# Scores with transposes or outputs behind them in one block of weights, and products' matmuls in written order

## The chip, the cores and the metric

The kernel runs on one core of a Trainium2 chip. The metric is the device time of one execution in microseconds, as the median of several runs. The engines that matter here are TensorE (PE in the profile, with its weight loads as PEld), VectorE (DVE), ScalarE (ACT), and SP, whose queue starts the transfers of the weights.

## The reference

A hybrid encoder of two layers on 256 tokens, width 2048, in float32. Cut to what matters:

```python
for i in range(DEPTH):                       # 2 layers
    h = rmsnorm(x, g_mix[i])
    z = h @ w_in[i]                          # dq, dk, dv, cq, ckv, kr, gate a, gate b
    # differential attention: 8 heads, two softmax maps of 64 columns each
    weights = softmax(q0 @ k0.T / 8) - lam * softmax(q1 @ k1.T / 8)
    od = rmsnorm(weights @ v, g_subln[i]) * (1 - lam_init)
    # latent attention: 8 heads, 128 + 64 (rotary) columns
    qf = rmsnorm(cq) @ w_q_up[i];  kvf = rmsnorm(ckv) @ w_kv_up[i]
    om = softmax((q_nope @ k_nope.T + q_rope @ k_rope.T) * scale) @ v_mla
    m = sigmoid(ga) * (od @ w_branch_diff[i]) + sigmoid(gb) * (om @ w_branch_mla[i])
    x = x + m @ w_out[i]
    x = x + (silu(g) * u) @ w_down[i]        # g, u = rmsnorm(x) @ w_gate_up[i], width 5632
    x = x + sigmoid(rmsnorm(x) @ w_ple_gate[i]) * (p[i] @ w_ple_in[i])
return rmsnorm(x, g_final)
```

## The kernel before, in words

Features lie on the 128 partitions and the 256 tokens along the free axis. A weight matrix is read from memory once per layer in pieces of 128 x 1024 floats (`piece`, at most eight blocks each), each of which ACT rounds to `whi` (L204) and DVE turns into the remainder `wlo` (L81, by the helper `tt`). Three buffers hold `whi` pieces and three `wlo` pieces. The activations are held the same way, as a hi and a lo half side by side in one tile of 512 columns: `ua` and `ub` are sixteen such tiles each.

A product of one output tile (`product`, or `pair` for two short ones) is a series of *blocks*, made in `emit`: for each input tile j a *lead*, hi weights times both halves of the tile (L229, 512 columns), and a *rest*, lo weights times the hi half (L233, 256 columns). Both add into one PSUM bank `mm`. Most products have 16 blocks. `blocks` lists the (lead, rest) pairs of a layer from the first queries on; it is emptied at that place in each layer.

The stages of a layer are: the values of the differential attention (`values`), the latents, queries and keys of eight heads with the attention of the heads before them (`pipelined`, with `beside` giving it products to fill in), latent attention with the gates as filling, the two branch products with `w_bd` and `w_bm`, `w_out`, the gated feed-forward in three parts of 14, 14 and 16 tiles (`FF_PARTS`), each followed by its share of `w_down`, and the last gate `w_pg`. `w_out` reads the merged tiles from `ua`, and `w_down` reads the feed-forward's tiles from `ua`. Every one of these tiles comes out of a short chain: ACT copies half of a bank (`joined`, L260), DVE adds the other half (L81), one or two DVE operations follow, and `split` writes the hi half by ACT (L268) and the lo half by DVE (L81).

Smaller matmuls stand among the blocks. Each head has scores S (L436, 12 matmuls of 64 rows for the differential heads, 10 of 128 rows for the latent ones), transposes of its weights T (L455, four), and outputs O (L729, four in the differential heads). N are the two matmuls that spread a norm over the partitions (L345). `settle` transposes the normalised outputs of a differential head, two transposes each (L745), and splits them. T, O, N and the transposes of `settle` write PSUM banks of the tag `at`, of which there are two; S writes banks of the tag `S`, also two.

The order of the instructions of each engine comes from a planner that simulates a timeline (`schedule_with_timeline_sim=True`) and takes what is ready first; dependencies without semaphores (`NO_SYNC`) can be added by hand to force an order on one engine. `PLACES` does so: an entry ("S", 6, 265) puts the scores of head 6 into block 265, that is behind its lead, ahead of its rest and ahead of the next block's lead. Between the entries of one block no order is given, and nothing else orders a block against the block before it.

`queries_keys(h, *inside)` can run a function inside step 8 of a product: the norms of the latents and, in `latent_norm`, the matmuls N.

Of the kernel before, what the change touches and what calls it, by code (L numbers as in the profile page):

```python
# [19 lines left out]
P = 128  # L20
T = 256
# [6 lines left out]
KVR = 256  # L28
# [14 lines left out]
GAPS = {("fa", 0): (8, 0), ("fc", 0): (48, 0), ("fa", 7): (0, 16)}  # L43
KR_GAP = 56
FIRST = 7
PLACES = (("N", 0, 24), ("N", 1, 56), ("S", 0, 65), ("S", 1, 112), ("T", 0, 112), ("S", 2, 148), ("T", 1, 148), ("S", 3, 176), ("T", 2, 176), ("S", 4, 210), ("T", 3, 210),
          ("S", 5, 234), ("T", 4, 234), ("O", 4, 240), ("S", 6, 265), ("O", 5, 272), ("T", 6, 296), ("S", 7, 297), ("T", 7, 337), ("O", 7, 361),
          ("S", 8, 416), ("S", 9, 432), ("T", 8, 438))
NO_SYNC = mybir.DependencyInfo(mybir.DependencyClass.NoSync, mybir.DependencyReason.DATA)

TWO_PI = 2.0 * math.pi
# [8 lines left out]
def encoder(ctx, tc, x, p, positions, cols, lams, wq, wk, wv, wcq, wckv, wkr, wga, wgb,  # L60
            w_q_up, w_kn, w_v, w_bd, w_bm, w_out, w_gate, w_up, w_down, w_pin, w_pg, rope_c, out):
    nc = tc.nc
    V, A, PE = nc.vector, nc.scalar, nc.tensor
# [10 lines left out]
    def scratch(tag, bufs, n=T):  # L74
        return tmp.tile([P, n], F32, tag=tag, name=tag, bufs=bufs)

    def bank(ps=ps_at, tag="at", name="at", shape=(P, 2 * T)):
        return ps.tile(list(shape), F32, tag=tag, name=name)

    def tt(o, a, b, op):  # L80
        return V.tensor_tensor(out=o, in0=a, in1=b, op=op)  # L81
# [8 lines left out]
    ua = [const.tile([P, 2 * T], F32R, name=f"ua{j}") for j in range(NC)]  # L90
# [27 lines left out]
    def g(name, i=0):  # L118
        return gcol[:, off[name] + i : off[name] + i + 1]


    ident = const.tile([P, P], F32, name="ident")
# [63 lines left out]
    def piece(src, n, high=0, low=0):  # L186


        w = wts.tile([P, PT * P], F32, tag="w32", name="w32", bufs=W_BUFS)
        lo = wts.tile([P, PT * P + 64], F32R, tag="wlo", name="wlo", bufs=3)[:, low : low + PT * P]  # L190
        if not step:
            step.append(wts.tile([P, STEP], F32, tag="step", name="step", bufs=1))
            nc.gpsimd.memset(step[0], 0.0)
        hi = wts.tile([P, PT * P + 64], F32R, tag="whi", name="whi", bufs=3)[:, high : high + PT * P]
        srcs = src if isinstance(src, list) else [src]
        m = n * P // len(srcs)
        for k, src in enumerate(srcs):
            dst = w[:, k * m : (k + 1) * m]
            if len(src.shape) == 3:
                dst = dst.rearrange("p (a b) -> p a b", a=src.shape[1])  # L200
            nc.sync.dma_start(dst, src)
        for k in range(len(srcs)):
            s = slice(k * m, (k + 1) * m)
            last_split[:] = A.activation(hi[:, s], w[:, s], AF.Copy), tt(lo[:, s], w[:, s], hi[:, s].bitcast(F32), ALU.subtract)  # L204
        if chores:
            with after_splits():
                chores.pop(0)()
        return hi, lo
# [8 lines left out]
    last_split, last_mm, chores, sq0, step, blocks = [], [], [], [], [], []  # L217
# [8 lines left out]
    def emit(acc, hi, lo, at, us, first, last, inside=None):  # L226
        for j, u in enumerate(us):
            s, start, stop = slice((at + j) * P, (at + j + 1) * P), first and j == 0, last and j == len(us) - 1
            lead = PE.matmul(acc, hi[:, s], u, start=start, stop=False)  # L229
            if inside and inside[0] == j:  # L230
                with tc.issue_after(lead.ins):
                    inside[1]()
            rest = PE.matmul(acc[:, T:], lo[:, s], u[:, :T], start=False, stop=stop)  # L233
            blocks.append((lead.ins, rest.ins))
            if inside and inside[0] == j:
                tc.keep_in_program_order(rest)

    def product(src, us, inside=None):


        acc = bank(ps_mm, "mm", "mm")
        n = len(us)
        for a in range(0, n, PT):
            m = min(PT, n - a)
            hi, lo = piece(src[:, a * P : (a + m) * P], m)
            emit(acc, hi, lo, 0, us[a : a + m], a == 0, a + m == n, inside and (inside[0] - a, inside[1]))
        return acc
# [10 lines left out]
    def joined(acc, o=None):  # L258
        t = scratch("join", 3)
        A.activation(t, acc[:, T:], AF.Copy)  # L260
        o = scratch("a", 4) if o is None else o
        tt(o, acc[:, :T], t, ALU.add)
        return o

    def split(u, src, gain=None):
        hi, lo = u[:, :T], u[:, T:]
        if gain is None:
            return A.activation(hi, src, AF.Copy), tt(lo, src, hi.bitcast(F32), ALU.subtract)  # L268
        return A.activation(hi, src, AF.Copy, scale=gain), stt(lo, src, gain, hi.bitcast(F32), ALU.mult, ALU.subtract)

    def rsqrt(src, n, eps, width):

        v, y, a = (stat.tile([P, 2 * DH], F32, tag="r" + s, name="r" + s, bufs=2)[:, :width] for s in "vya")
        ts(v, src, 1.0 / n, eps, ALU.mult, ALU.add)
        ts(y.bitcast(I32), v.bitcast(I32), -0.5, 1597463007.0, ALU.mult, ALU.add)
        for _ in range(3):
            stt(a, y, -0.5, y, ALU.mult, ALU.mult)
            tt(a, a, v, ALU.mult)
            stt(y, a, 1.5, y, ALU.add, ALU.mult)
        return y  # L280
# [52 lines left out]
    def norm(sums, n):  # L333

        s = bank()
        for j, a in enumerate(sums):
            for b in range(2):
                PE.matmul(s[:, b : b + 1], a[:, b * P : (b + 1) * P], ones[:, 0:1], start=j + b == 0, stop=j + b == len(sums))
        return rsqrt(s[:, 0:2], n, EPS, 2)
# [130 lines left out]
    def weights(tag="E", dt=F32):  # L470
        return tmp.tile([P, 2, T], dt, tag=tag, name=tag, bufs=2)

    groups = {"N": [], "S": [], "T": [], "O": []}

    def place(kind, n, block):


        lead, rest = blocks[block]
        for i in groups[kind][n]:
            for late, early in ((i, lead), (rest, i), (blocks[block + 1][0], i)):  # L480
                tc.add_manual_dep(late, early.name, NO_SYNC, reason="inside a block")

    last_exp = [None]
    SWAP16 = [(j + 16) % 32 for j in range(32)]
# [62 lines left out]
    for L in range(DEPTH):  # L547
# [44 lines left out]

        def queries_keys(h, *inside):
            for which, w in enumerate((wq, wk)):
                a = joined(product(w[L, h], ua, inside=(8, inside[which]) if inside and inside[which] else None))
                sh = scratch("sh", 2)
                V.stream_shuffle(sh, a, ROPE16)
                tt(sh, sh, sr, ALU.mult)
                tt(a, a, cr, ALU.mult)
                tt(a, a, sh, ALU.add)  # L600
                split(qk[h][which], a)


        cq, ckv = ub[8:12], ub[12:14]
# [9 lines left out]
        def latent_norm(us, gain, raws, col, behind=False):  # L614
            rl = spread(col, behind)
            for c in range(len(us)):
                stt(raws[c], raws[c], g(f"{gain}{L}", c), rl, ALU.mult, ALU.mult)
                split(us[c], raws[c])
# [20 lines left out]
        rq, rkv = raws[:4], raws[4:]  # L639
        skv = latent(ckv, wckv, rkv)  # L640
        sq = latent(cq, wcq, rq)
        lcols = []

        def norm_and_latent(sq):
            lcols.append(norm([sq], QR))
            latent_norm(ckv, "g_kv_latent", rkv, lcols[0], True)

        blocks.clear()
        for group in groups.values():
            group.clear()  # L650
        queries_keys(0, lambda: lcols.append(norm([skv], KVR)), lambda: norm_and_latent(sq))
        queries_keys(1, None, lambda: latent_norm(cq, "g_q_latent", rq, lcols[1]))

        def beside():

# [40 lines left out]
        gas, gbs, early = [], [], []  # L696
# [40 lines left out]
        def settle(h0):  # L737

            rd = rsqrt(ssd[:, 2 * h0 : 2 * h0 + 8], P, SUB_EPS, 8)
            for h in range(h0, h0 + 4):  # L740
                t = bank()
                for b in range(2):
                    o, j = od[h][:, b * P : (b + 1) * P], 2 * (h - h0) + b
                    ts(o, o, rd[:, j : j + 1], None, ALU.mult)
                    PE.transpose(t[:, b * P : (b + 1) * P], o, ident)  # L745
                split(ods[h], t[:, :T], gsub[:, L : L + 1])

        def pipelined(weigh, put, heads, step):
# [38 lines left out]
            split(oms[h], o[:, :T])  # L787

        pipelined(mla_weights, mla_out, MH, fill_gate)
        for kind, n, block in PLACES:  # L790
            place(kind, n, block)

        for n in todo:
            gate(wgb, gate_b, n - NC)
# [28 lines left out]
        for part, (f0, f1) in enumerate(FF_PARTS):  # L823
            for f in range(f0, f1):
                a = pre.pop(0) if pre else joined(product(w_gate[L, f], ub))
# [5 lines left out]
                b = pre.pop(0) if pre else joined(product(w_up[L, f], ub))  # L831
# [26 lines left out]
        for n in range(NC - 2 * final):  # L858
            a = pre.pop(0) if pre else joined(product(w_pg[L, n], ub))
# [15 lines left out]
    parts, banks, tiles_ = {}, {}, {}  # L875
# [14 lines left out]
    for n in ends:  # L890
        m = banks[n, 1] = bank(ps_mm, "mm", "mm")
        for j in range(whole[n], NC):
            w = slice(j % PT * P, (j % PT + 1) * P)
# [185 lines left out]
```

## Time and profile before

| | |
|---|---|
| median of 3 runs | 2825.02 us (2824.64 to 2825.53) |
| profiled execution, its own time | 2824.55 us |
| its span in the profile | 2822.7 us, 43984 instructions |
| mean granted clock of TensorE | 1.00 |
| DVE busy | 2079.6 us, 74% |
| ACT busy | 1533.2 us, 54% |
| matmuls of L229, on ub and on ua | 3936 and 3712 |
| HBM read | 526.39 MB, 187 GB/s over the span |

A row of the timeline has the start and the duration in us from the span's start, the engine, the line, the operation, what it writes and reads by the program's names without numbers, its shape and how many are merged into the row. In brackets stands the idle time ahead of it and what ended it, where there was any. Starts of PE rows are recorded; their ends are modelled and overlap the next start. A row of the wait list has the waiter, what it waited for, us in total, times, and the longest.

### The profile page before, as it was taken

The numbers are of one execution on the slowest core, as the hardware profiler recorded it, in microseconds if no ns is written. First come the engines' busy times: TensorE is split into PE (matmuls) and PEld (weight loads), VectorE is DVE, ScalarE is ACT, GpSimd is POOL, SyncE is SP. The second block draws the span as 40 slices with busy tenths as digits, with TensorE's granted clock in tenths as the row PEclk, the third lists the DMA queues.
The fourth block names the chain that finished last, engine by engine and source line by source line (L and its number), as shares of the span: only waits on it lengthen the run. The fifth ranks groups of instructions, "written<-read, shape, count | busy, mean of one in ns | idle before, by whom it ended". The sixth has DMA issues, their size and how long they took to land.

```text
span 2822.7 us, 43984 instructions
## 1 busy us (share of the span) xinstructions
PE 2815.3 (100%) x16691; PEld 2490.4 (88%) x16691; DVE 2079.6 (74%) x3566; ACT 1533.2 (54%) x2554; POOL 3.1 (0%) x17
## 2 busy tenths in 40 slices
PE   9999999999999999999999999999999999999999
PEld 8888988888888888888888889888888888888888
DVE  8898668776666666677869976687766666666777
ACT  7676546554444444455646765465544444444555
POOL 0000000000000000000000000000000000000000
PEclk9999999999999999999999999999999999999999
DMA  7545455555665565565564454555556655655664
GB/s 247 175 162 172 158 186 198 193 194 194 187 200 193 188 194 198 193 194 193 195 192 167 157 172 158 193 198 193 194 194 189 199 193 184 202 194 193 193 193 157
DMA packets 158180, 531.36 MB, mean 188 GB/s; under 512 B 17168, under 2 KB 25360, under 8 KB 157968
## 3 DMA queue, kind: packets, MB, share of 16 engines
q1 hardware_dynamic: 157536, 527.96, 56.8%
q8 instruction: 131, 2.15, 0.3%
q10 hardware_dynamic: 432, 0.59, 0.1%
q14 instruction: 81, 0.66, 0.1%
HBM read 526.39 MB, written 2.10 MB: 187 GB/s over the span
## 4 chain that ended last, share of the span: by engine, by line
PE 100%; DVE 0%; DVEq 0%; issue 0%
PE mm L229 61%; PE mm L233 31%; PE S L436 1%; PE mmv L522 1%; PE mmv L523 1%; PE mmv L521 1%; PE at L455 1%; PE at L729 1%; PE mm L878 0%; PE at L786 0%; PE mm L422 0%; PE at L537 0%; PE at L745 0%; PE mmv L492 0%; PE at L345 0%; PE at L311 0%
## 5 line engine op out<-in xcount | busy, mean ns | idle before, releaser
L204 ACT ACTIVATE whi<-w 128x1024 fp32r<-128x1024 f32 (+2 forms) x1038 | 1064.1, 1026 | 1209.5 <-issue 576.6
L81 DVE TENSOR_TENSOR wlo<-w,whi 128x1024 fp32r<-128x1024 f32 (+2 forms) x1038 | 1225.2, 1181 | 638.1 <-ACT whi L204 627.8
L229 PE MATMUL mm<-ub,whi 128*128 128x512 f32 x3936 | 1339.6, 389 | 0.0
L229 PE MATMUL mm<-ua,whi 128*128 128x512 f32 x3712 | 1273.6, 390 | 0.0
L233 PE MATMUL mm<-ub,wlo 128*128 128x256 f32 x3936 | 1086.5, 276 | 0.0
L233 PE MATMUL mm<-ua,wlo 128*128 128x256 f32 x3712 | 1028.5, 278 | 0.0
L229 PEld LDWEIGHTS mm<-ub,whi 128*128 128x128 f32 x3936 | 737.9, 188 | 152.0
L229 PEld LDWEIGHTS mm<-ua,whi 128*128 128x128 f32 x3712 | 696.2, 188 | 140.6
L233 PEld LDWEIGHTS mm<-ub,wlo 128*128 128x128 f32 x3936 | 738.7, 188 | 1.0
L233 PEld LDWEIGHTS mm<-ua,wlo 128*128 128x128 f32 x3712 | 696.9, 188 | 2.1
L81 DVE TENSOR_TENSOR a<-mm,join 128x256 f32<-128x256 f32 (+1 forms) x423 | 174.0, 416 | 1.7 <-ACT join L907 1.4
L260 ACT ACTIVATE join<-mm 128x256 f32<-128x256 f32 x452 | 165.6, 369 | 4.0 <-PE mm L233 3.4
L81 DVE TENSOR_TENSOR xT<-xT,mm 128x256 f32<-128x256 f32 x256 | 106.8, 420 | 41.5 <-PE mm L233 37.6
L81 DVE TENSOR_TENSOR a<-a,row 128x256 f32<-128x256 f32 (+1 forms) x209 | 87.8, 421 | 6.0
L81 DVE TENSOR_TENSOR a<-a 128x256 f32<-128x256 f32 x120 | 51.0, 425 | 4.0
L81 DVE TENSOR_TENSOR ua<-a,ua 128x256 fp32r<-128x256 f32 x120 | 50.1, 417 | 1.0 <-ACT ua L268 1.0
L446 ACT ACTIVATE E<-S,nm 128x256 f32<-128x256 f32 x96 | 44.2, 473 | 11.9 <-DVE nm L87 11.6
L268 ACT ACTIVATE ua<-a 128x256 fp32r<-128x256 f32 x120 | 48.4, 404 | 2.6 <-DVE a L81 2.6
L521 PE MATMUL mmv<-whi,ua 128*128 128x512 f32 x124 | 47.0, 391 | 0.0
L522 PE MATMUL mmv<-whi,ua 128*128 128x512 f32 x124 | 47.0, 392 | 0.0
L523 PE MATMUL mmv<-wlo,ua 128*128 128x512 f32 x124 | 41.2, 391 | 0.0
L81 DVE TENSOR_TENSOR ssq<-ssq,sq 128x256 f32<-128x256 f32 x96 | 40.0, 417 | 0.3 <-ACT sq L298 0.3
(214 smaller groups left out, 1209.6 us busy)
## 6 DMA issues: line engine op xcount, KB each, us to landing
w<-in_w_gate SPq DMA_DIRECT2D x176, 512.0 KB, 4.6
w<-in_w_up SPq DMA_DIRECT2D x176, 512.0 KB, 4.6
w<-in_w_down SPq DMA_DIRECT2D x128, 512.0 KB, 4.2
w<-in_wga SPq DMA_DIRECT2D x64, 512.0 KB, 3.8
w<-in_wgb SPq DMA_DIRECT2D x64, 512.0 KB, 3.7
w<-in_w_out SPq DMA_DIRECT2D x64, 512.0 KB, 4.5
w<-in_w_pg SPq DMA_DIRECT2D x64, 512.0 KB, 4.6
w<-in_w_down SPq DMA_DIRECT2D x64, 384.0 KB, 3.6
```

The lines of the kernel that those rows point to most:

```text
L81: return V.tensor_tensor(out=o, in0=a, in1=b, op=op)
L204: last_split[:] = A.activation(hi[:, s], w[:, s], AF.Copy), tt(lo[:, s], w[:, s], hi[:, s].bitcast(F32), ALU.subtract)
L229: lead = PE.matmul(acc, hi[:, s], u, start=start, stop=False)
L233: rest = PE.matmul(acc[:, T:], lo[:, s], u[:, :T], start=False, stop=stop)
L260: A.activation(t, acc[:, T:], AF.Copy)
L268: return A.activation(hi, src, AF.Copy), tt(lo, src, hi.bitcast(F32), ALU.subtract)
L436: group.append(PE.matmul(S[:, b, :], q[:, b * P : (b + 1) * P], k, start=j == 0, stop=j == len(pairs) - 1).ins)
L446: last_exp[0] = A.activation(E[:, b, :], S[:, b, :], AF.Exp, bias=nm[:, b : b + 1], scale=scale, accum_out=sm[:, b : b + 1])
L455: group.append(PE.transpose(tp[:, kb, b * P : (b + 1) * P], W[:, b, kb * P : (kb + 1) * P], ident).ins)
L521: PE.matmul(banks[k][b], xh, hi[:, s], start=c == 0, stop=False)
L522: PE.matmul(banks[k][b], xl, hi[:, s], start=False, stop=False)
L523: last_mm[:] = [PE.matmul(banks[k][b], xh, lo[:, s], start=False, stop=c == n - 1)]
```

## The change

It has three parts. `emit` adds two dependencies without semaphores per block, so that each lead stands behind the rest of the block written before it, and each rest behind its own lead, through the whole program; `blocks` is no longer emptied, and each layer counts from `base`. `PLACES` becomes a table from block to names, and `place` strings the names of a block in the order given: lead, first name, second name, ..., rest. And the entries differ: S0 goes from block 65 to 59 and N1 from 56 to 59 behind it; S6 from 265 and O5 from 272 to 268 together; T6 from 296 to 297 behind S7 and ahead of F0; F4 to F7 (the transposes of `settle`, which had no place) to 424, 425, 432 and 435; S10 and T9, which had none, to 480. The function inside the second head's keys runs at step 11 instead of 8.

```diff
-PLACES = (("N", 0, 24), ("N", 1, 56), ("S", 0, 65), ("S", 1, 112), ("T", 0, 112), ("S", 2, 148), ("T", 1, 148), ("S", 3, 176), ("T", 2, 176), ("S", 4, 210), ("T", 3, 210),
-          ("S", 5, 234), ("T", 4, 234), ("O", 4, 240), ("S", 6, 265), ("O", 5, 272), ("T", 6, 296), ("S", 7, 297), ("T", 7, 337), ("O", 7, 361),
-          ("S", 8, 416), ("S", 9, 432), ("T", 8, 438))
+PLACES = {24: ["N0"], 59: ["S0", "N1"], 112: ["S1", "T0"], 148: ["S2", "T1"], 176: ["S3", "T2"], 210: ["S4", "T3"], 234: ["S5", "T4"],
+          240: ["O4"], 268: ["S6", "O5"], 297: ["S7", "T6", "F0"], 337: ["T7"], 361: ["O7"], 416: ["S8"], 424: ["F4"], 425: ["F5"],
+          432: ["F6", "S9"], 435: ["F7"], 438: ["T8"], 480: ["S10", "T9"]}
...
             rest = PE.matmul(acc[:, T:], lo[:, s], u[:, :T], start=False, stop=stop)
+            if blocks:
+                behind(lead.ins, blocks[-1][1])
+            behind(rest.ins, lead.ins)
             blocks.append((lead.ins, rest.ins))
...
-    groups = {"N": [], "S": [], "T": [], "O": []}
-
-    def place(kind, n, block):
+    groups = {k: [] for k in "NSTOF"}
+
+    def behind(late, early):
+        tc.add_manual_dep(late, early.name, NO_SYNC, reason="order of matmuls")
+
+    def place(block, names):
         lead, rest = blocks[block]
-        for i in groups[kind][n]:
-            for late, early in ((i, lead), (rest, i), (blocks[block + 1][0], i)):
-                tc.add_manual_dep(late, early.name, NO_SYNC, reason="inside a block")
+        parts = [lead, *(i for name in names for i in groups[name[0]][int(name[1:])])]
+        for early, late in zip(parts, parts[1:]):
+            behind(late, early)
+        behind(rest, parts[-1])
+        behind(blocks[block + 1][0], parts[-1])
...
-        blocks.clear()
+        base = len(blocks)
         for group in groups.values():
             group.clear()
-        queries_keys(0, lambda: lcols.append(norm([skv], KVR)), lambda: norm_and_latent(sq))
-        queries_keys(1, None, lambda: latent_norm(cq, "g_q_latent", rq, lcols[1]))
+        queries_keys(0, (8, lambda: lcols.append(norm([skv], KVR))), (8, lambda: norm_and_latent(sq)))
+        queries_keys(1, None, (11, lambda: latent_norm(cq, "g_q_latent", rq, lcols[1])))
...
-                t = bank()
+                t, group = bank(), []
...
-                    PE.transpose(t[:, b * P : (b + 1) * P], o, ident)
+                    group.append(PE.transpose(t[:, b * P : (b + 1) * P], o, ident).ins)
+                groups["F"].append(group)
...
-        for kind, n, block in PLACES:
-            place(kind, n, block)
+        for block, names in PLACES.items():
+            place(base + block, names)
```

More of the change, by code (lines that the diff above doesn't have):

```diff
@@ L594, in queries_keys @@
             for which, w in enumerate((wq, wk)):
-                a = joined(product(w[L, h], ua, inside=(8, inside[which]) if inside and inside[which] else None))
+                a = joined(product(w[L, h], ua, inside=inside[which] if inside else None))
                 sh = scratch("sh", 2)
```

## The prediction, made before the changed kernel was seen

> **What bounds the kernel now.** I read the page's busy table first, then the chain, the waits of TensorE, and the timeline of PE, DVE and ACT, stage by stage. The first fence has the PE row, its granted clock, and the only row of the wait list that has PE as the waiter.
>
> ```profile
> PE 2815.3 (100%) x16691; PEld 2490.4 (88%) x16691; DVE 2079.6 (74%) x3566; ACT 1533.2 (54%) x2554; POOL 3.1 (0%) x17
> PEclk9999999999999999999999999999999999999999
> PE at L537 <- DVE ones L126: 1.1, 1, 1.1
> ```
>
> PE is busy from end to end and never waits after its warm-up. So the time is the sum of the distances from one matmul's start to the next. PE rows overlap (a lead "takes" 0.39 us, but the next starts 0.23 later), so I price by starts, not by durations. Two things can change the time: distances between neighbours, and waits that PE does not have today.
>
> **Where the order is not the written one.** A block is a lead (L229, 512 columns, hi weights) and a rest (L233, 256 columns, lo weights). The second fence is the start of w_out's products in layer 0: PE rows turn from ub to ua. ACT and DVE rows of the same stretch stand between them.
>
> ```profile
> 504.24 0.28 PE L233 MATMUL mm<-ub,wlo 128*128 128x256 f32 x1
> 504.35 0.39 PE L229 MATMUL mm<-ua,whi 128*128 128x512 f32 x1
> 508.17 0.40 ACT L268 ACTIVATE ua<-a 128x256 fp32r<-128x256 f32 x1
> 508.30 1.23 DVE L81 TENSOR_TENSOR wlo<-w,whi 128x1024 fp32r<-128x1024 f32 x1 [0.24 <-ACT whi L204]
> 509.44 0.42 DVE L81 TENSOR_TENSOR ua<-a,ua 128x256 fp32r<-128x256 f32 x1
> 509.45 0.39 PE L229 MATMUL mm<-ua,whi 128*128 128x512 f32 x1
> 512.85 0.62 PE L229 MATMUL mm<-ua,whi 128*128 128x512 f32 x2
> 513.31 0.39 PE L233 MATMUL mm<-ua,wlo 128*128 128x256 f32 x2
> 513.54 0.40 PE L229 MATMUL mm<-ua,whi 128*128 128x512 f32 x1
> ```
>
> Fifteen blocks take 509.45 - 504.35 = 5.10 us, 0.340 each. The sixteenth of w_out's first product reads the last ua, the split of the last merged tile. Its lo half ends at 509.44 + 0.42 = 509.86; the sixteenth block would start at 509.45. The planner put it later: at 512.85 two leads stand side by side and at 513.31 two rests. That is one block of the first product inside the second's eleventh, (512.85 - 504.35) / 0.340 = 25 blocks in. So PE today fills a hole with the next product. The change forbids this: each lead stands behind the rest written before it.
>
> **What the written order costs.** By the same reading, at the starts of the other stages that consume freshly split tiles: w_down's first part (14 tiles, so 13 blocks before the last), its third (16 tiles), and the last such place of layer 1; then a start where the tile is early, w_down's second part. (Rows are picked out of the timelines of PE and DVE.)
>
> ```profile
> 744.02 0.39 PE L229 MATMUL mm<-ua,whi 128*128 128x512 f32 x1
> 748.63 0.42 DVE L81 TENSOR_TENSOR ua<-a,ua 128x256 fp32r<-128x256 f32 x1
> 1233.75 0.39 PE L229 MATMUL mm<-ua,whi 128*128 128x512 f32 x1
> 1238.84 0.42 DVE L81 TENSOR_TENSOR ua<-a,ua 128x256 fp32r<-128x256 f32 x1
> 2636.78 0.39 PE L229 MATMUL mm<-ua,whi 128*128 128x512 f32 x1
> 2641.87 0.42 DVE L81 TENSOR_TENSOR ua<-a,ua 128x256 fp32r<-128x256 f32 x1
> 972.63 0.39 PE L229 MATMUL mm<-ua,whi 128*128 128x512 f32 x1
> 975.40 0.42 DVE L81 TENSOR_TENSOR ua<-a,ua 128x256 fp32r<-128x256 f32 x1 [0.48 <-ACT ua L268]
> ```
>
> - w_out: 509.86 - 509.45 = 0.41 us of waiting.
> - w_down, first part: due at 744.02 + 13 x 0.340 = 748.44, ready at 749.05: 0.61.
> - w_down, third part: due at 1233.75 + 5.10 = 1238.85, ready at 1239.26: 0.41. The last row pair, layer 1, gives the same: 2641.88 and 2642.29.
> - w_down, second part: due at 972.63 + 4.42 = 977.05, ready at 975.82; no wait. The first products of the gate and of the ple gate read ub, whose last tile is a sum and one split, without the merge or the sigmoid; on the same reading they wait for nothing.
>
> PE runs in order, so nothing behind the waiting lead can start, and no other engine gains from it. That is 1.43 per layer, **+2.86 us** for two. How fast PE wakes isn't shown: a DVE row may start 0.09 before the one ahead of it ends (509.44 against 508.30 + 1.23), and the dearest entry to a matmul below costs 0.09, so each wait is good to about 0.1, 0.6 in all. I take 0, the middle.
>
> By the Trainium skill, page "TensorE: Matmul & The Clock Gate", section "Part 2: What happens when you issue a matmul", only weight loads are pulled ahead in PE's queue, while matmuls keep program order. By that rule the 2.86 is paid in full; if the engine itself went past a waiting matmul, it would be 0, which is the first rival's sum. The trace agrees as far as it goes: the displaced blocks stand where the program put them.
>
> What the order gives back: from 512.85 to 513.54 two blocks take 0.69 instead of 0.68. Each displaced block costs 0.01 to 0.04; I find about a dozen such places in a layer (leads or rests in pairs), and at 0.02 this is **-0.48 us** for both layers (bounds 0 and -1.0). The other displaced blocks stand in the attention part, one lead or half a weight pair early. Following their operands through the timeline, I find each one written 1.0 us or more before its block in written order, so they are taken at 0.
>
> **What the places cost.** A run's cost is the distance between the leads around it, less 0.340. The rows: scores of head 6 alone; S1 with T0 behind it; T8 alone; T6 with the two F0 transposes; an F pair between blocks, two blocks in all.
>
> ```profile
> 192.34 0.39 PE L229 MATMUL mm<-ua,whi 128*128 128x512 f32 x1
> 192.66 0.98 PE L436 MATMUL S<-fa,ub 64*128 64x256 f32 x12
> 193.80 0.39 PE L229 MATMUL mm<-ua,whi 128*128 128x512 f32 x1
> ...
> 123.62 0.39 PE L229 MATMUL mm<-ua,whi 128*128 128x512 f32 x1
> 123.94 0.97 PE L436 MATMUL S<-fa,ub 64*128 64x256 f32 x12
> 124.84 0.66 PE L455 MATMUL at<-ident,E 128*128 128x128 f32 x4
> 125.46 0.39 PE L229 MATMUL mm<-ua,whi 128*128 128x512 f32 x1
> ...
> 267.03 0.39 PE L229 MATMUL mm<-ua,whi 128*128 128x512 f32 x1
> 267.82 0.39 PE L229 MATMUL mm<-ua,whi 128*128 128x512 f32 x1
> ...
> 204.97 0.39 PE L229 MATMUL mm<-ua,whi 128*128 128x512 f32 x1
> 205.97 0.39 PE L229 MATMUL mm<-ua,whi 128*128 128x512 f32 x1
> ...
> 209.17 0.40 PE L229 MATMUL mm<-ua,whi 128*128 128x512 f32 x1
> 209.52 0.38 PE L745 MATMUL at<-ident,fa 128*128 128x128 f32 x2
> 210.09 0.40 PE L229 MATMUL mm<-ua,whi 128*128 128x512 f32 x1
> ```
>
> S alone 1.46 - 0.34 = 1.12; T alone 0.45; S with T 1.50: together they save 0.07, say 0.06. Entering S costs 192.66 - 192.34 = 0.32 where a rest would start after 0.23: the 0.09 used above. T6 with F0 costs 0.66, so an F pair behind another transpose costs 0.21 against 0.92 - 0.68 = 0.24 by itself.
> - S1/T0 to S5/T4, N0, O4, T7, O7, S8, T8 keep their blocks: 0.
> - N1 joins S0 (block 59), O5 joins S6 (268), S7 joins T6 and F0 (297): three joins per layer. S before N or O isn't in the trace; nearest is S before T, 0.06. Bounds 0 and 0.11 (a rest behind S is followed at 0.22 by its lead, not 0.11). I take 0.06: **-0.36 us** over both layers.
> - F6 behind block 432's lead with S9: -0.03 per layer, **-0.06**. F4, F5 and F7 cost 0.24 wherever they stand; F1 to F3 stay free. S10 with T9 moves from between two products into block 480: 0, within 0.05.
> - The latent norm's N1 goes from step 8 to step 11 of its product and behind S0: about 2 us later for the ACT and DVE work on cq, which the query-up products read only a hundred blocks on. S0's operands are split before its new place too, six blocks (2.0 us) ahead of the old. No instruction, transfer or semaphore is added; the new dependencies are all on one engine. The weight transfers on SP and POOL's queue are not passed by anything.
>
> **Sum.** 2.86 - 0.48 - 0.36 - 0.06 = +2.0 us on the profiled execution's 2824.55, so 2826.5; the median of the runs shown, 2825.02, is 0.47 above that execution, so the forecast is **2827.0 us**. A change under 0.2%, 5.65 us, can't be told from none: below 2819.4 is faster, above 2830.7 slower.
>
> **The rivals.**
> 1. *The waits don't come.* At 508.57 the hi half is done, but DVE is in a wlo split until 509.53. If the planner, now that PE stands, puts ua's lo half ahead of that split, it ends near 509.0 and PE waits nowhere. Against: the two orders are planned alike up to that block. Time: 2825.0 - 0.9 = 2824.1. Chance 0.18.
> 2. *Slower: one more weight split in front of the last tile.* The trace already has one wlo split between its two halves; the planner believed the tile 10 blocks late, so its timeline is not the chip's. If in its new order another split of 1.23 us goes ahead at each of the six starts, PE waits 1.23 longer there: +7.4, so 2834.4. It decides once the six waits average (5.65 + 0.9) / 6 = 1.09 us. For it: the DVE row at 508.30 stands in the way already. Against: nothing in the change moves DVE's work before them. Chance 0.12.
> 3. *A bank wait at T8.* F6 and F7 now stand 6 and 3 blocks ahead of T8, and `at` has two banks:
>
> ```profile
> 254.50 0.27 PE L745 MATMUL at<-ident,fa 128*128 128x128 f32 x1
> 256.93 0.48 DVE L84 SCALAR_TENSOR_TENSOR ub<-at,gsub,ub 128x256 fp32r<-128x256 f32 x1
> ```
>
> F4 holds its bank for 2.9 us. From F6 to T8 there are 6 x 0.34, scores of about 1.1 and two transpose pairs of 0.2, some 3.6 us. If F6 is held 1 us longer than F4, PE waits 0.3; if it is 1.5 longer, 0.8: at most +1.6 for two layers, 2828.6. Chance 0.07.
> 4. *Faster.* If scores left no penalty at all: 0.09 in, 0.09 and 0.11 behind, 0.29 for 16 heads, 4.7 us, and only six runs are changed. That is under 5.65 even so. Chance 0.03.
>
> The forecast keeps 0.60. The range goes from rival 1 less the runs' spread of 0.9 (2823.4) to the forecast with 0.6 of waking, rival 3's 1.6 and one extra split at one start per layer, 2 x 1.23 (2831.7). Rival 2 and rival 4 stay outside. Faster 0.03, same 0.85, slower 0.12.
>
> **What would show it.** PE rows: no two leads side by side; at the first products of w_out and of w_down's first and third part the sixteenth (fourteenth) lead stands 0.4 to 0.6 us late, and the wait list gets a group "PE mm L229 <- DVE ua L81" (lines shifted) of some 2.9 us in six waits. S with T6 and F0 behind it costs near 1.71 instead of 1.12 + 0.66. PE waits of over a microsecond there would be rival 2; none at all, rival 1; a wait of L455 for an ACT or DVE reader of `at`, rival 3. Waits anywhere in the attention part would mean that planned slack was not as I read it.

## The result, and the profile after

The changed kernel takes 2850.33 us in the median of 12 runs (2827.73 to 2863.68); the kernel before 2825.08 in 12 (2824.24 to 2826.14). The ratio is 1.0083, 95% interval 1.006 to 1.0106: slower, by more than the forecast's whole range. As telling as the median is the spread, 36 us against 2. The fastest run is within a microsecond of the forecast of 2827.0, but that is luck and no support for it: the next one stands at 2835.03.

The profiled execution took 2853.53 us, span 2851.7, 29.0 more than the 2822.7 before. The page's busy row, and from the list of waits the rows of PE and PEld that wait for the last tile (waiter, releaser: us in total, times, longest):

```profile
PE 2840.3 (100%) x16691; PEld 2502.0 (88%) x16691; DVE 2083.4 (73%) x3566; ACT 1532.8 (54%) x2554; POOL 3.1 (0%) x17
```

```profile
PE mm L229 <- DVE ua L81: 2.1, 6, 0.4
PEld mm L229 <- DVE ua L81: 4.0, 6, 0.8
```

The six waits are there, at the six places named. But they are idle time, 2.1 us of it, and the PE row has grown by 25.0 (2815.3 to 2840.3) with the same 16691 instructions. So most of the 29.0 is not waiting: PE is busy longer with the same work. The rest of the span is 1.9 us of a later end of the last stores, which nothing in the change touches and which stays unexplained.

Here is one wait in PE's timeline (start, length, operation), the sixteenth block of w_out's first product in layer 0:

```profile
509.33 0.39 PE L229 MATMUL mm<-ua,whi 128*128 128x512 f32 x1
509.56 0.28 PE L233 MATMUL mm<-ua,wlo 128*128 128x256 f32 x1
510.13 0.50 PE L229 MATMUL mm<-ua,whi 128*128 128x512 f32 x1 [0.30 <-DVE ua L81]
510.47 0.28 PE L233 MATMUL mm<-ua,wlo 128*128 128x256 f32 x1
510.59 0.40 PE L229 MATMUL mm<-ua,whi 128*128 128x512 f32 x1
510.82 0.28 PE L233 MATMUL mm<-ua,wlo 128*128 128x256 f32 x1
510.94 0.40 PE L229 MATMUL mm<-ua,whi 128*128 128x512 f32 x1
511.17 0.28 PE L233 MATMUL mm<-ua,wlo 128*128 128x256 f32 x1
```

Read by starts: the lead comes 0.57 behind the rest instead of 0.11, so the wait costs 0.46, and its own rest comes 0.34 behind it instead of 0.23, another 0.11. That is all that the forecast looked for, and it ends at 510.59. The next leads, though, start at 510.59, 510.94 and (not shown) 511.29: 0.350 apart, where blocks ahead of the wait were 0.340 apart. And it does not stop. The grouped view of the same gate and up products in the kernel before (count, duration in ns min/median/max, first and last start):

```profile
L229 PE MATMUL mm<-ub,whi x384: 389/389/389, 609.7 to 739.9; 128*128 128x512 f32 x192
L233 PE MATMUL mm<-ub,wlo x383: 276/276/276, 609.9 to 739.8; 128*128 128x256 f32 x192
```

and in the changed kernel, first in the same stretch, then behind the next wait:

```profile
L233 PE MATMUL mm<-ub,wlo x373: 279/279/282, 609.8 to 740.0; 128*128 128x256 f32 x187
L229 PE MATMUL mm<-ub,whi x372: 395/395/395, 609.9 to 739.7; 128*128 128x512 f32 x186
...
L229 PE MATMUL mm<-ub,whi x925: 389/389/389, 828.7 to 1229.9; 128*128 128x512 f32 x185
L233 PE MATMUL mm<-ub,wlo x924: 276/276/276, 828.9 to 1229.7; 128*128 128x256 f32 x185
```

130.2 us / 383 is 0.340 a block; 129.8 / 371 is 0.350. Every lead of the slow stretch has 395, every lead of the fast one 389: PE has two steady beats and keeps one of them for hundreds of blocks. In this execution the slow one holds from the w_out wait to the w_down part 1 wait (258 + 441 blocks) and from the part 3 wait to the layer's end (258 + 236; 258 + 212 in layer 1), in both layers alike; behind the part 1 waits the beat is fast. That is 2362 blocks, 23.6 us at 0.010. Both kernels also have short slow stretches, in the attention stage above all. Counted over the whole span (leads 0.346 to 0.354 apart), there are 2566 slow blocks here and 294 in the kernel before, 22.7 us more. The waits add 3.07, the late rest behind each 0.65, and the later end of the stores 1.9; 0.7 lies scattered.

A wait also ends the slow beat: the part 1 wait is reached at 0.350 and left at 0.340. And not every other matmul in the stream ends it: the two of a norm (L314, at 601.12) stand between the 258 slow blocks and the 441.

### The profile page after: what moved, and what is told of

Its sections match the earlier page's. It is cut to its first block, busy times and chain, and to the rows that moved or that the text cites. A ratio compares the mean times of both kernels' runs of the same rounds, so it can differ in the third digit from the quotient of the medians.

```text
span 2851.7 us, 43986 instructions
## 1 busy us (share of the span) xinstructions
PE 2840.3 (100%) x16691; PEld 2502.0 (88%) x16691; DVE 2083.4 (73%) x3566; ACT 1532.8 (54%) x2554; POOL 3.1 (0%) x17
## 4 chain that ended last, share of the span: by engine, by line
PE 99%; DVE 0%; issue 0%; ACT 0%; DVEq 0%
PE mm L229 61%; PE mm L233 31%; PE S L439 1%; PE mmv L529 1%; PE mmv L531 1%; PE mmv L530 1%; PE at L458 1%; PE at L737 1%; PE mm L887 0%; PE at L795 0%; PE mm L425 0%; DVE wlo L81 0%; ACT whi L204 0%; PE at L545 0%; PE mmv L500 0%
## 5 line engine op out<-in xcount | busy, mean ns | idle before, releaser
L229 PE MATMUL mm<-ub,whi 128*128 128x512 f32 x3936 | 1354.1, 391 | 0.0
```

## The experiments

My theory after reading the two traces: a wait can leave PE in the slow beat, which lasts until PE is disturbed again; before, nothing waited. The rivals: the new places do it; the chain of dependencies does it by itself; it is drawn by chance whatever stands ahead; or PE loses SBUF access to the other engines.

**The places alone** (changed kernel, chain taken out).

```diff
-            if blocks:
-                behind(lead.ins, blocks[-1][1])
-            behind(rest.ins, lead.ins)
```

> The changed kernel with its new places for S, T, O, F and N and its order within a block, but without the dependencies that tie each block of weights to the block before it. The planner is then free again to put the last block of a product behind later ones, as before, and PE should not wait at the six stage starts. Theory (the waits leave PE in a slower beat, 350 ns a block instead of 340, until something else disturbs it): no long slow stretch, 2822 to 2826 us, all runs within 2 us. Rival A (the new places themselves bring the slow beat): as the changed kernel, about 2850 us with runs spread over 2828 to 2864. Rival B (the chip was slower in those runs, at any order): 2850 us too, and the kernel before beside it spread as widely.

Measured: 2826.32 (2825.58 to 2827.73, 11 runs), before 2825.01, ratio 1.0004 (0.9995 to 1.0012). No long slow stretch (the longest has 42 blocks): rivals A and B fall. The median is 0.3 above the expected range. Part of that is seen: the places alone let one rest wait for its lo weights in each layer (120.61 to 121.40 in PE's timeline where 0.23 is usual, 0.56 more):

```profile
PE mm L233 <- DVE wlo L81: 0.8, 2, 0.4
```

**The chain alone** (kernel before, with the three lines above added).

> The kernel before with one part of the change alone: the dependencies that keep the weights' matmuls in their written order; the places of S, T, O, N stay as before. Theory: the six waits of 0.46 or 0.61 us come at the starts of w_out and of w_down parts 1 and 3 (3 us together, and 0.65 us for the block behind each), and after each the beat can be 350 ns a block: about 700, 1440 and 490 blocks in each layer at 10 ns, 6.8 + 14 + 4.8 us per layer when all are slow; so 2828 us without any slow stretch and up to 2880 with all, runs spread over some 2828 to 2864. Rival A (the places bring it): 2828 us with runs within 2 us. Rival C (the waits cost only their own length): 2828 us, and no stretch of blocks with a mean other than 340 ns in the profile.

Measured: 2849.46 (2840.37 to 2870.97, 6 runs), ratio 1.0092 (1.0065 to 1.0118). The chain by itself brings the whole loss; rivals A and C fall. Its profile has the six waits and slow stretches of 258 + 441 and 1440 blocks in layer 0, none in layer 1:

```profile
PE mm L229 <- DVE ua L81: 2.1, 6, 0.5
```

**The chain without its waits** (changed kernel, the waiting block left loose).

```diff
-            if blocks:
-                behind(lead.ins, blocks[-1][1])
+            free = loose and last and j == len(us) - 1
+            if order and not free:
+                behind(lead.ins, order[-1])
             behind(rest.ins, lead.ins)
+            if not free:
+                order.append(rest.ins)
...
-            accumulate(n, product(w_out[L, n], ms))
+            accumulate(n, product(w_out[L, n], ms, loose=n == 0))
...
-                accumulate(n, product(w_down[L, n][:, f0 * P : f1 * P], ua[: f1 - f0]))
+                accumulate(n, product(w_down[L, n][:, f0 * P : f1 * P], ua[: f1 - f0], loose=n == 0 and part != 1))
```

> The changed kernel, but the last block of the first product of w_out and of the two parts of w_down that wait (three a layer, six in all) is left out of the chain, so that it may run later, as in the kernel before; all other matmuls stay in written order. Theory: with the six waits the slow stretches behind them go too: 2822 to 2826 us, runs within 2 us, and the stretches of w_out and w_down at 340 ns a block. Rival D (the chain as a whole, not the waits, makes PE slower, since each matmul must follow another): stays near 2850 with the spread.

Measured: two groups and nothing between them, six runs at 2823.60 to 2825.07 and six at 2842.93 to 2843.63. Half a miss: the waits are gone and the slow beat still comes, in half of the runs. The profiled one, of the upper group, shows where; layer 0 first, then the same stretch of layer 1:

```profile
L229 PE MATMUL mm<-ub,whi x948: 389/389/389, 821.0 to 1230.0; 128*128 128x512 f32 x190
...
L229 PE MATMUL mm<-ub,whi x900: 395/395/395, 2225.5 to 2629.7; 128*128 128x512 f32 x180
```

In layer 1 it begins at w_down part 1, where the loose block runs between the two matmuls of another (two leads, two rests), and holds for 1439 + 247 + 212 blocks: 19.0 us, the distance of the groups. So a wait isn't needed: a change in the alternation can do it too. It does so seldom: of the six loose blocks in this profile four led to no more than four slow blocks, and one stood in the slow beat already. And the chain as a whole is not slow: in half of the runs it is as fast as before.

**Transposes behind the wait.**

```diff
+    def four():
+        t = bank()
+        for b in range(4):
+            tc.keep_in_program_order(PE.transpose(t[:, b * P : (b + 1) * P], ident, ident))
...
-            accumulate(n, product(w_out[L, n], ms))
+            accumulate(n, product(w_out[L, n], ms, inside=(NC - 1, four) if n == 0 else None))
```

(and the same in the first products of w_down parts 1 and 3).

> The changed kernel with four added transposes of the identity, whose output nobody reads, between the two matmuls of each of the six blocks that wait; the waits stay. Theory (the beat lasts until something else disturbs it, and transposes in a block leave the fast one, as they do in the attention stage): six waits as before, 3.7 us, and six groups of four transposes at about 0.45 us, 2.7 us; no slow stretch behind them: 2828 to 2832 us, runs within 3 us. Rival C (the beat has nothing to do with what disturbed PE last; it is drawn anew in each run): spread of 2830 to 2866 us as in the changed kernel, median near 2853.

Measured: 2845.64 (2835.75 to 2850.22, 6 runs). A miss: less spread than the changed kernel, but not 2828 to 2832. In the profiled run (2844.42) five of six groups were followed by the fast beat, and the sixth by 1440 slow blocks, 14.4 us; without them it would be 2830.0. Leads from 2156.93 on are 0.350 apart:

```profile
2155.68 0.51 PE L229 MATMUL mm<-ua,whi 128*128 128x512 f32 x1 [0.50 <-DVE ua L81]
2156.02 0.60 PE L244 MATMUL at<-ident 128*128 128x128 f32 x4
...
2156.58 0.39 PE L229 MATMUL mm<-ua,whi 128*128 128x512 f32 x1
...
2156.93 0.40 PE L229 MATMUL mm<-ua,whi 128*128 128x512 f32 x1
...
2157.28 0.40 PE L229 MATMUL mm<-ua,whi 128*128 128x512 f32 x1
```

Transposes do not reset the beat reliably. That they do anything to it isn't shown either: waits without them were followed by the fast beat in 10 of 18 cases (counted below).

**A disturbance without a wait**: 12 matmuls of 64 rows in the kernel before, then the same with four transposes behind them.

```diff
+    def halves64():
+        Ss = [bank(ps_s, "S", "S", (P, 2, T)) for _ in range(2)]
+        for b in range(2):
+            for j in range(3):
+                for d in (1, 0):
+                    s = slice(d * 64, d * 64 + 64)
+                    tc.keep_in_program_order(PE.matmul(Ss[d][:, b, :], krs[1][s, b * P : (b + 1) * P], krs[0][s, :T], start=j == 0, stop=j == 2))
...
-                accumulate(n, product(w_down[L, n][:, f0 * P : f1 * P], ua[: f1 - f0]))
+                accumulate(n, product(w_down[L, n][:, f0 * P : f1 * P], ua[: f1 - f0], inside=(4, halves64) if n == 4 and part == 0 else None))
```

> The kernel before with 12 added matmuls of 64 rows, whose output nobody reads, inside one block of the fifth product of w_down part 1, in each layer; no dependency is added that makes PE wait. They cost about 1.2 us each time by what the same 12 take in the attention stage, 2.4 us together. Theory (any disturbance can leave PE in the slower beat, a wait is only one of them, and the beat stays until the next): after them 350 ns a block until the end of w_down part 2, some 1390 blocks a layer, 14 us each: 2827 us if both stretches are fast, 2841 with one slow, 2855 with both; the times stand in such steps. Rival (only a wait for another engine brings it): 2827 us, all runs within 2 us, no long stretch at 350 ns.

> The run with 12 added matmuls of 64 rows, and four added transposes of the identity behind them in the same block (output unread). If transposes reset the beat in most cases (five of the six groups did where they stood behind a wait): 2828 us in most runs, steps of 14 us above it in some. If what stands last does not matter: the same mixture as without the transposes, 1 us higher.

Measured: 2827.20 (2826.73 to 2828.10) and 2828.30 (2827.78 to 2828.62), 10 runs each, before 2825.18. No steps in either; the 1400 blocks or so behind are at 0.340 in both layers of both profiles. A miss for the theory: not every disturbance does it. The rival, that only a wait does it, is not saved by this, since the run with the waiting blocks loose had shown otherwise; and with no slow stretch to reset, the second kernel tells nothing of resetting.

**The chain in the attention stage only** (the three lines hold from the first q/k product to the last of w_bm).

```diff
+            if chained[0]:
+                if blocks:
+                    behind(lead.ins, blocks[-1][1])
+                behind(rest.ins, lead.ins)
...
+        chained[0] = True
         for group in groups.values():
...
+        chained[0] = False
         acc, add = stream(ub, f"g_ffn{L}")
```

> The changed kernel with the written order kept only from the first q/k product to the last of w_bm; w_out and all products behind it are ordered by the planner again, as before. Theory: the joined places and the written order in the attention stage are worth what their own rows say (the wait of 0.75 us a layer that the places alone showed goes, the joins give about 0.3 us a layer), and with no wait behind w_bm no long slow stretch: 2823 to 2825 us, runs within 2 us, at or just under the kernel before. Rival (the chain makes PE slower wherever it stands): 2830 or more with a spread.

Measured: 2824.38 (2824.00 to 2825.67, 11 runs), before 2825.18, ratio 0.9998 (0.9989 to 1.0007). As the theory had it: all the harm is done behind w_bm. A gain can't be told from none.

**Is it PE or its neighbours?** One kernel before and one changed, with an eighth of the weight traffic in w_down part 2.

```diff
+            nc.sync.dma_start(dst[:, :width] if width else dst, src[:, :width] if width else src)
...
+            s = slice(k * m, k * m + (width or m))
...
+            s, start, stop = slice(0, P) if one else slice((at + j) * P, (at + j + 1) * P), first and j == 0, last and j == len(us) - 1
```

> The run with 12 added matmuls of 64 rows, and in w_down part 2 (224 blocks a layer) each piece of weights loads and splits only its first block, which all blocks of the piece then use: the products there are of other numbers, with an eighth of the DMA and of the splits on DVE and ACT. Theory (the beat belongs to PE): if the stretch before w_down part 2 runs at 350 ns a block, those 224 blocks do so too, and in a layer where it runs at 340 they run at 340. Rival (the slower beat is PE losing SBUF access to the splits and the weights' DMA): those 224 blocks come to 340 ns or less whatever the stretch before them had.

> The changed kernel, waits and all, but in w_down part 2 (224 blocks a layer) each piece of weights loads and splits only its first block, which all blocks of the piece use: the products there are of other numbers, with an eighth of the weights' DMA and of the splits on ACT and DVE. It needs a layer in which the stretch behind the wait of w_down part 1 came out slow (in the profiles of the changed kernel and of the chain alone one of four). Theory (the beat is PE's own): the 224 light blocks keep the beat of the stretch before them, 350 behind 350. Rival (the slow beat is PE losing SBUF access to splits and DMA): the light blocks come down to 340 ns or less, and the blocks behind them go back up.

One run of each. The first (2827.74, on the kernel with 64-row matmuls) had no slow stretch ahead of the light blocks and so decides nothing. The second (2856.20) came out slow behind both part 1 waits. Windows ahead of, in and behind the light blocks of layer 0 (length; busy us and instructions of PE, PEld, DVE, ACT and POOL; clock, DMA share, GB/s):

```profile
760.00:960.00 200.00, 200.00 (x1145) 175.09 (x1144) 130.44 (x184) 90.42 (x122) 0.00 (x0) 1.00 0.61 190
990.00:1045.00 55.00, 55.00 (x315) 48.11 (x315) 20.48 (x55) 12.35 (x34) 0.00 (x0) 1.00 0.17 48
1070.00:1240.00 170.00, 170.00 (x974) 148.85 (x973) 113.58 (x166) 81.60 (x120) 0.00 (x0) 1.00 0.58 189
```

and the leads of the middle window:

```profile
L229 PE MATMUL mm<-ua,whi x158: 394/395/396, 989.8 to 1044.8; 128*128 128x512 f32 x158
```

DMA falls from 0.61 to 0.17, DVE from 65% to 37%, ACT from 45% to 22%, the clock stays 1.00, and the beat stays: 55.0 / 157 = 0.350. So contention for SBUF does not keep the slow beat up, and neither does the clock. Whether contention has a part in starting it isn't tested: the waits themselves stood under the full load.

**Setting the beat by order alone.** The kernel before holds a hint: at w_down part 1 it goes through ten slow blocks, until an extra lead ends them (x2 is two leads side by side).

```profile
755.67 0.40 PE L229 MATMUL mm<-ua,whi 128*128 128x512 f32 x1
...
756.02 0.40 PE L229 MATMUL mm<-ua,whi 128*128 128x512 f32 x1
...
756.37 0.62 PE L229 MATMUL mm<-ua,whi 128*128 128x512 f32 x2
756.83 0.28 PE L233 MATMUL mm<-ua,wlo 128*128 128x256 f32 x1
756.94 0.39 PE L229 MATMUL mm<-ua,whi 128*128 128x512 f32 x1
757.17 0.28 PE L233 MATMUL mm<-ua,wlo 128*128 128x256 f32 x1
757.28 0.39 PE L229 MATMUL mm<-ua,whi 128*128 128x512 f32 x1
```

0.350 ahead of the pair, 0.340 behind it. The extra lead is the first of the fourth product, six blocks early; the chain takes it out. It is no single case. In the kept traces a pair of leads with one rest behind it follows ten or more slow blocks eleven times (this one; five in the kernel with the places alone, two of them behind 42 slow blocks; two in the one with 64-row matmuls; one each in three others), and each time the blocks behind are fast. Two leads with two rests are another matter: such a pair began the slow stretch of the kernel with loose blocks, and another inside that stretch (at 2659.84) did not end it. Two kernels put one back. The first is the run with the waiting blocks loose, and that pair:

```diff
+            parts = [lead.ins, rest.ins]
+            if ahead and last:
+                held.extend(parts if j else parts[1:])
+                parts = [] if j else parts[:1]
+            elif held:
+                parts[1:1], held[:] = held, []
...
+                accumulate(n, product(..., loose=n == 0 and part != 1, ahead=n == 2 and part == 0))
```

> The run with the last blocks left free (its times stood at 2824 or 2843, by one stretch of w_down part 1 that locked in at 350 ns), with one more change of order: the first matmul of w_down part 1's fourth product runs six blocks early, between the two matmuls of the third product's ninth block, as the planner has it in the kernel before; all else stays in the chain. Theory (the beat is drawn anew at each change of the alternation, and an extra 512-column matmul at this place led to 340 ns in each profile in which it stands): 2823.5 to 2825 us in all runs, no second group at 2843. Rival (the chain behind it lets the slow beat in again, wherever): still two groups 19 us apart.

Measured: 2824.57 (2823.23 to 2824.81, 11 runs), before 2824.83; no second group, where half of the runs without the pair were 19 us higher. Those were taken on another chip, so this comparison alone leaves the chip as a rival. (In its profile the slow beat at this place had already ended by itself, after four blocks; what the pair does to it is seen in the next kernel.)

The second is the changed kernel, waits and all, with a block of the second product drawn apart behind each wait:

```diff
+            order = [lead.ins, rest.ins]
+            if late and last and j == len(us) - 1:
+                held[:], order = order, []
+            elif held and first and j == 2:
+                order.insert(1, held.pop(0))
+            elif held and first and j == 7:
+                order.append(held.pop())
...
```

> The changed kernel with its six waits, and behind each of them one more change of order: of the last block of the second product, the 512-column matmul runs between the two of the third product's third block and the 256-column one behind the third product's eighth block. No work is added. Theory (the waits stay, 3.7 us; the extra 512-column matmul 15 blocks behind sets the beat to 340 ns): 2827 to 2829 us, runs within 2 us, six waits in the profile and no long stretch at 350. Rival (what sets the beat is the wait alone and nothing in the order resets it): as the changed kernel, 2828 to 2864 with a median near 2850.

Measured: 2828.29 (2827.58 to 2829.23, 11 runs), before 2824.83, ratio 1.0012 (1.0003 to 1.0021). The waits, then the timeline behind one of them:

```profile
PE mm L229 <- DVE ua L81: 2.2, 6, 0.5
```

```profile
749.81 0.50 PE L229 MATMUL mm<-ua,whi 128*128 128x512 f32 x1 [0.50 <-DVE ua L81]
...
750.26 0.40 PE L229 MATMUL mm<-ua,whi 128*128 128x512 f32 x1
...
755.16 0.40 PE L229 MATMUL mm<-ua,whi 128*128 128x512 f32 x1
755.39 0.28 PE L233 MATMUL mm<-ua,wlo 128*128 128x256 f32 x1
755.51 0.62 PE L229 MATMUL mm<-ua,whi 128*128 128x512 f32 x2
755.97 0.28 PE L233 MATMUL mm<-ua,wlo 128*128 128x256 f32 x1
756.09 0.39 PE L229 MATMUL mm<-ua,whi 128*128 128x512 f32 x1
756.31 0.28 PE L233 MATMUL mm<-ua,wlo 128*128 128x256 f32 x1
756.42 0.39 PE L229 MATMUL mm<-ua,whi 128*128 128x512 f32 x1
```

This wait left the slow beat: from 750.26 to 755.51 there are 15 blocks of 0.350. Then two leads stand side by side, and from 756.09 the blocks are 0.340 apart, for more than 1400 blocks. It is the only one of the six that did so in this profile; behind the others at most three blocks were slow. The six waits are as long as in the changed kernel; no work was added or taken away; and 22 us of median and 34 us of spread are gone.

## Why the prediction was wrong, point by point

- *"PE is busy from end to end ... distances between neighbours, and waits"*: the right frame. I then took the distance of blocks in steady flow as one number.
- *"Fifteen blocks take 509.45 - 504.35 = 5.10 us, 0.340 each"*: **the step that failed.** True of those fifteen, and used for all, before and after the change. The sum has no term for a changed distance in steady flow; the runs showed 0.350 over 2362 blocks, 23.6 of the 29.0 us. A difference of 0.010 looks like rounding in one block and is 14 us over 1440. The trace of the kernel before held 294 such blocks: ten in a row at w_down part 1, and over thirty in a row in the attention stage of each layer (leads; durations in ns and starts as above):

```profile
L229 PE MATMUL mm<-ua,whi x31: 395/395/395, 108.3 to 118.8; 128*128 128x512 f32 x31
```

- *The six waits, +2.86*: they came, at these places, for this reason. By starts 0.46, 0.61 and 0.46 per layer, 3.07, and 0.11 more for the rest behind each: 3.72. With the 0 that I took for waking, each wait with the rest behind it was 0.11 to 0.16 short, where the bound was 0.1. The kernel with the beat reset, less the one with the chain in the attention stage only, gives 2828.29 - 2824.38 = 3.9, which agrees within the runs' noise.
- *What a wait can cost*: I bounded it by its length and its waking. What follows a wait was put at nothing, without a reason. In the changed kernel that was the larger part by six to one (22.7 against 3.7).
- *"Each displaced block costs 0.01 to 0.04"*: I counted the displaced blocks as a small loss that the written order gives back. The one that stands as an extra lead at w_down part 1 ended a slow stretch; in the chain with loose blocks, which lacks it, half of the runs kept the slow beat for the next 1400 blocks and more.
- *The joins and F6, -0.42, and the order's -0.48*: by starts the three joins saved 0.02 to 0.05 each instead of 0.06. The kernel with the chain in the attention stage stands 0.8 below the one before, within its interval of 2.5 either way, so neither term is measured beyond its rows. That the places without the chain cost 1.3 more was not foreseen.
- *The range*: rival 1 less the spread is 2824.1 - 0.9 = 2823.2, not 2823.4; nothing hangs on it.
- *The rivals*: the waits came (first), no second split stood in front of a tile, as the longest wait was 0.61 (second), and nothing waited at T8 (third). The result ended on the second rival's side by another mechanism.
- *The rule of the Trainium skill that matmuls keep program order* (page "TensorE: Matmul & The Clock Gate", section "Part 2: What happens when you issue a matmul"): the trace agrees. No matmul went past a waiting lead, and the lead's own weight load came as late as the lead (4.0 us of PEld in the list above).

**The mechanism as shown.** Chaining removes the freedom that kept PE from waiting and from staying slow; the chain alone gives the whole loss, and order alone takes all but some 4 us of waiting away. **Open**: what in PE holds the beat, and why one wait leaves it and the next does not. Of 18 waits in three profiles (changed kernel, chain alone, light blocks) 8 led into a long slow stretch, and waits of the same 0.46 us led to either. Six of the 18 came in the slow beat, and five of these ended it. So a wait seems to draw the beat anew rather than only to slow it; what decides the draw, no run shows. Nothing beat both kernels: the two fastest stand at 0.9998 of the kernel before, intervals 0.9989 to 1.0007.

## What to carry to other kernels

When an engine is busy all the time, take its steady distance from several stretches of the trace and to the nanosecond, before trusting one; a grouped view with minimum and maximum shows two beats at a glance (389/389/389 against 395/395/395). Price a new wait by what it may leave behind as well as by its length, above all at the head of a long undisturbed stretch. And look at the spread of the runs first: a kernel whose runs fall into groups, 2824 or 2843, holds a state that is drawn anew in each run, and the distance of the groups divided by the price of a block tells how long it lasts.

## What the runs showed of the hardware

- An alternating stream of 512-column and 256-column matmuls with new weights for each has two steady beats on PE, 0.340 and 0.350 us a pair, at a granted clock of 1.00 in both. Each of the two matmuls is some 5 ns later. By the Trainium skill, page "TensorE: Matmul & The Clock Gate", section "Wait — 56ns, not 53.3ns?", a warm matmul follows the one ahead after its columns at 2.4 GHz and some 2.5 ns; an estimate from this is 325 ns for the pair. Neither beat agrees, so here the measured ones decide.
- The slow beat, once there, did not change with the load of DMA, DVE and ACT: 0.350 at a DMA share of 0.61 and of 0.17 (one run).
- After a wait, the rest of the waiting block started 0.34 behind its lead instead of 0.23.
- Two 512-column matmuls side by side with one 256-column matmul behind them ended the slow beat in eleven of eleven cases where ten or more slow blocks stood ahead; with two 256-column ones behind them they did not in the one case on record. Four transposes behind a wait did not always leave the fast beat (5 of 6), and 12 matmuls of 64 rows in the planner's order never brought the slow one (four stretches of some 1400 blocks in two profiles; no step in 20 runs).
